# Expert input rows by indirect DMA and transposes instead of gather products, with the gate tiles and the identity moved within SBUF

## The chip, the cores and the metric

The kernel runs on one core of a Trainium2 chip, as one program. The metric is device time in microseconds (us) of one execution, as the median of several runs; lower is better. The core has five engines with a queue each: TensorE (PE, matrix products; its loads of the stationary operand are listed apart as PEld), VectorE (DVE), ScalarE (ACT), GpSimd (POOL) and SyncE (SP, which here only issues DMAs). SBUF is the on-chip memory of 128 partitions; PSUM receives PE's results in banks.

## What is computed

A two-layer trunk on 256 tokens of width 1024 in float32. Layer 0 is a gated spatial mixer followed by a dense SwiGLU. Layer 1 is an attention mixer followed by the part that matters here, a mixture of eight experts where each token goes to two:

```python
def moe_swiglu(x, w_router, w_in, w_out):
    logits = (xt @ w_router)                       # xt: 256 tokens x 1024, RMS-normed
    top_v, top_i = lax.top_k(logits, TOP_K)        # 2 of 8
    top_w = jax.nn.softmax(top_v, axis=-1)
    gates = sum(one_hot(top_i, N_EXPERTS) * top_w) # 256 x 8
    for e in range(N_EXPERTS):
        y = y + gates[:, e:e+1] * swiglu(xt, w_in[e], w_out[e])
```

`w_in[e]` is 1024 x 7168 and `w_out[e]` 3584 x 1024. The eight experts' weights are some 350 of the 459 MB that the program moves.

## The kernel before

**Products in two parts.** All products are made to keep float32 accuracy: each operand is split into a high part (a cast to fp32r) and a low part (the rest), and `mm3` (lines 167 to 171) issues three matmuls, high x weight high (L169), high x weight low (L170), low x weight high (L171). The tokens are the stationary operand (128 x 128), the weights the moving one (128 x 512).

**Weights.** `Stream` fetches weights in units of 128 x 2048 (1 MB) into `w_raw` tiles, issued by SP (L75), up to 9 units ahead in the expert stage. Two halves of each unit are split by ACT (`w_hi`, L91) and DVE (`w_lo`, L100) into a ring of six pairs, from which PE reads. `w_raw` and the other large tiles share one pool of 14 buffers (`big`).

**Experts.** Each expert has a capacity of 128 slots here (a second pass for more than 128 tokens of one expert is behind a branch that is not taken in these runs). `slot` holds the place of each token in each expert. An expert has 14 steps `j`, each over 256 columns of the hidden width: 24 matmuls `mm<-w,xg` (8 chunks of 128 of the input width, three each), SwiGLU on ACT and DVE (`silu` L604, `glu` L605), two transposes of `glu` of the step before (L1177, by the identity tile `ident`), their split into `mgh` on ACT (L1170) and `mgl` on DVE (L1171), and 12 matmuls `acc<-w,mg` into the expert's output. A step reads three units of weights. Program order is written by hand, and every engine works through its queue in that order.

**Input of an expert.** `choose(p)` writes `pick`, the 0/1 matrix (256 tokens x 2 x 128 slots) of a pair of experts, with four DVE instructions (L1128). `gather(p, k)` makes two of the eight chunks of the input of both experts, already transposed: eight matmuls (L1141) with the two parts of the normed tokens (`xnh`, `xnl`) as stationary operand and `pick` moving, 256 columns each, then a cast on ACT (`xgh`, L1144) and a subtraction on DVE (`xgl`, L1145). Four calls make a pair. `slot_info(e)` multiplies `pick` of one expert with `info` (two tiny matmuls, L1150) and so gets each slot's gate, reciprocal norm and token number (`si`, `sg`, L1154 and L1155), and `put` (L1156), a 0/1 matrix of which only the last expert's is read.

**Where these stand.** They go into a list `side`. `pop_side` takes one entry after the 24 `mm` matmuls of a step, one after the first six `acc` matmuls and one after the second six. At step 3 of an odd expert the list gets `choose`, four `gather` and `slot_info` for the next pair, at step 3 of an even expert `slot_info` alone.

**Rows through device memory.** Outputs of experts 0 to 6 are written to a table in device memory (`rows_of`), and four indirect DMAs issued by POOL (`fetch`, L1202) bring each token's two rows back, behind expert 6.

**Before the experts.** `last_out` finishes the attention output, makes the normed tokens `xn` (half 0, then half 1), and calls `parts_of(xn, t)` (lines 966 to 973), which squares `h` on ACT (L316) into a scratch that then receives `xnh`, and makes `xnl`. These tiles are of a pool of four buffers; `xnh` of half 1 takes the buffer that `xn` of half 0 had.

**Addresses.** Nearly all tiles that PE reads start at byte 32 of a 256-byte block of a partition (the large tiles, the weight parts, `gh` and `gl` of the dense layer). `ident`, `mgh` and `mgl` start at byte 160. `phase(nc, pool, size)` allocates padding to set this.

Of the kernel before, what the change touches and what calls it, by code (L numbers as in the profile page):

```python
# [12 lines left out]
F32 = mybir.dt.float32  # L13
F32R = mybir.dt.float32r
# [7 lines left out]
P = 128  # L22
D = 1024
KT = D // P
T = 256
# [97 lines left out]
def phase(nc, pool, size):  # L123


    nc.gpsimd.memset(pool.tile([P, size // 4], F32, name="phase"), 0.0)
# [3 lines left out]
def trunk(ctx: ExitStack, tc: tile.TileContext, a, out):  # L130
# [18 lines left out]
    def aux_bank():  # L149
        return ps_aux.tile([P, 512], F32, name="aux", tag="aux")  # L150
# [4 lines left out]
    def big(dt, name):  # L155
        return bigp.tile([P, BIG], dt, name=name, tag="big")
# [7 lines left out]
    def tok(t):  # L164
        return slice(t * P, (t + 1) * P)
# [83 lines left out]
    units += moe_units(True)  # L249
    ws = Stream(nc, bigp, parts_pool, units, 6)  # L250

    ident = const.tile([P, P], F32, name="ident")
    make_identity(nc, ident)

    wr = const.tile([P, KT * NE], F32, name="wr")
    wr2 = const.tile([P, KT, 2 * NE], F32R, name="wr2")

    def count_up(shape, pattern, base, step, name):
        t = const.tile(shape, F32, name=name)
        nc.gpsimd.iota(t, pattern, base=base, channel_multiplier=step, allow_small_or_imprecise_dtypes=True)  # L260
        return t

    iota_e = count_up([P, NE], [[1, NE]], 0, 0, "iota_e")
    iota_1 = count_up([P, T], [[1, T]], 1, 0, "iota_1")
    number = count_up([P, TT], [[P, TT]], 1, 1, "number")
    strict = const.tile([P, P], BF16, name="strict")
    ones = const.tile([P, P], BF16, name="ones")
    nc.gpsimd.memset(strict, 1.0)
# [37 lines left out]
        for f in todo:  # L306
            f()

    ssh = const.tile([P, TT], F32, name="ssh")
    spare = const.tile([P, 1], F32, name="spare")  # L310
    nc.vector.memset(spare, 0.0)

    def square(t, room=None):
# [647 lines left out]


    xns = {}

    def parts_of(xn, t):

        hi = xnp.tile([P, D], F32R, name="xnh", tag="xn")
        square(t, hi)
        nc.scalar.copy(hi, xn)
        pool, tag = (gains, "gain") if t else (xnp, "xn")  # L970
        lo = pool.tile([P, D], F32R, name="xnl", tag=tag)
        nc.vector.tensor_sub(lo, xn, hi.bitcast(F32))
        xns[t] = hi, lo
# [3 lines left out]
    ws.set_depth(11)  # L977
    pa = ctx.enter_context(tc.tile_pool(name="ma", bufs=1))
    pb = ctx.enter_context(tc.tile_pool(name="mb", bufs=2))
    phase(nc, pa, 64)  # L980
    gate = pa.tile([P, TT, NE], F32, name="gate")
    o1 = pa.tile([P, TT, NE], F32, name="o1m")
    chosen = pa.tile([P, TT, NE], BF16, name="chosen")
# [11 lines left out]
    mostf = pa.tile([P, 1], F32, name="mostf")  # L995
    rm = pa.tile([P, TT], F32, name="rm")
    rms = pa.tile([P, TT, 2], F32R, name="rms")
    s2 = pa.tile([P, TT, 2], F32, name="s2")
    at_row = pa.tile([P, TT, 2], F32, name="at_row")
    fit = pa.tile([P, TT, 2], F32, name="fit")  # L1000
# [1 line left out]
    o1s = pa.tile([P, TT, NE], F32, name="o1s")  # L1002
    place = [pa.tile([P, TT, 2], I32, name=f"place{i}") for i in range(2)]
    nc.gpsimd.memset(nil, 0.0)
    dram = ctx.enter_context(tc.tile_pool(name="dram", bufs=1, space=bass.MemoryType.DRAM))
    nc.gpsimd.memset(info.bitcast(F32), 0.0)


# [105 lines left out]
    def experts(ws, base, before):  # L1114
# [3 lines left out]

        slots = iota_1[:, base : base + P]
        pick, xgs, slot_gate, put, ys, ym, first = {}, {}, {}, {}, {}, {}, {}  # L1120

        def choose(p):

# [6 lines left out]
        def gather(p, k, bank=aux_bank):  # L1130
# [13 lines left out]
            nc.scalar.copy(gh, ps)  # L1144
            nc.vector.tensor_sub(gl, ps, gh.bitcast(F32))  # L1145

        def slot_info(e):
            ps = aux_bank()[:, :6]
            for t in range(TT):
                nc.tensor.matmul(ps, pick[e // 2][:, t, e % 2], info[:, t, e], start=t == 0, stop=t == TT - 1)  # L1150
            si = pb.tile([P, 6], F32, name="si", tag="si")
            slot_gate[e] = pb.tile([P, 2], F32, name="sg", tag="sg")
            put[e] = pb.tile([P, T], F32R, name="put", tag="put")
            nc.vector.tensor_copy(si, ps)  # L1154
            nc.vector.tensor_add(slot_gate[e], si[:, 0:2], si[:, 2:4])  # L1155
            nc.vector.tensor_scalar(put[e], iota_1, si[:, 4:5], None, op0=ALU.is_equal)  # L1156

        def slot_rms():

            ps = aux_bank()[:, :2]  # L1160
            for t in range(TT):
                nc.tensor.matmul(ps, pick[0][:, t, 0], rms[:, t], start=t == 0, stop=t == TT - 1)
            slot_gate[0] = pb.tile([P, 2], F32, name="sg", tag="sg")
            phase(nc, pb, 32)
            nc.vector.tensor_reduce(slot_gate[0][:, 1:2], ps, AX.X, ALU.add)

        def in_parts(pt):
# [115 lines left out]
        for s in range(1 if before else 0, NE * NJ):  # L1283
# [8 lines left out]
                side.append(lambda: slot_info(0))  # L1292
                side.append(lambda: places(0))
            if j == 3 and e < NE - 1:
                if e % 2 == 1:
                    p = e // 2 + 1
                    side.append(lambda p=p: choose(p))
                    side.extend(lambda p=p, k=k: gather(p, k) for k in range(0, KT, 2))
                side.append(lambda e=e: slot_info(e + 1))
            final = s == NE * NJ - 1  # L1300
            for q in range(4):
                w = ws.take(limit=4 if final else N_PARTS)
                for k2 in range(2):
                    k = 2 * q + k2
                    x = tuple(g[:, k, cs] for g in xgs[e // 2])
                    mm3(ps, x, cols(w, k2 * 512, (k2 + 1) * 512), k == 0, k == KT - 1)
                if q == 0 and s == 2 and before:
                    gT0 = first_rows()
                if q == 1 and prev is not None:
                    gT = transposed_m(prev[3])  # L1310
                if q == 3:
                    pop_side()
# [85 lines left out]
```

## Time and profile before

| | us |
|---|---|
| median of 3 runs (1568.2 to 1569.3) | 1568.31 |
| profiled execution, its own time | 1570.13 |
| span of its records | 1567.8 |
| PE busy | 1547.5 |
| DVE busy | 1271.3 |
| ACT busy | 1058.1 |

The profiled execution took 1.8 us more than the median, and 2.3 us of it lie outside its span. The expert stage runs from about 586 us to the end, and PE's granted clock is 1.00 of full speed in it. In the rows, the start of an instruction is in us from the span's start; a matmul's recorded duration includes its way through the array, so that successive matmuls overlap. The distance from one start to the next is what a matmul costs PE.

### The profile page before, as it was taken

How to read it: one execution, taken by the hardware profiler on the slowest of the kernel's cores; microseconds unless marked ns; L12 is line 12 of the kernel's file. 1: busy time of each engine (PE TensorE's matmuls, PEld its weight loads, DVE VectorE, ACT ScalarE, POOL GpSimd, SP SyncE). 2: the span in 40 equal slices, each digit the busy share in tenths (PEclk: the TensorE clock that was granted, in tenths of full speed). 3: DMA queues.
4: the chain of work that ended last, by engine and by line, in shares of the span. 5: the costliest groups of instructions: out<-in, count | busy, mean ns of one | idle time of the engine just before them, and what ended most of it. 6: DMA issues, size and time to landing. Idle time of an engine off the chain costs nothing.

```text
span 1567.8 us, 20336 instructions
## 1 busy us (share of the span) xinstructions
PE 1547.5 (99%) x7389; PEld 1288.3 (82%) x7389; DVE 1271.3 (81%) x1636; ACT 1058.1 (67%) x1403; POOL 48.4 (3%) x76
## 2 busy tenths in 40 slices
PE   9999999999999999999999999999999999999997
PEld 8999988888889777888888888888888888888875
DVE  6576666555786679999999999999999998998996
ACT  6555544444556657777777777777778777777774
POOL 1000000000100520000000000000000000000100
PEclk9999999999999999999999999999999999999999
DMA  9465648552333558998999998999998999999980
GB/s 379 138 208 194 237 174 339 184 188 81 126 148 135 189 215 319 377 365 316 352 371 367 419 385 315 342 367 361 420 385 314 349 374 383 372 412 338 396 355 29
DMA packets 70172, 459.30 MB, mean 293 GB/s; under 512 B 8032, under 2 KB 10096, under 8 KB 19376
## 3 DMA queue, kind: packets, MB, share of 16 engines
q1 hardware_dynamic: 67104, 451.97, 75.5%
q10 hardware_dynamic: 2160, 3.68, 0.6%
q0 software_dynamic: 800, 2.28, 0.5%
q8 instruction: 60, 0.98, 0.3%
q14 instruction: 48, 0.39, 0.1%
HBM read 453.17 MB, written 4.72 MB: 292 GB/s over the span
## 4 chain that ended last, share of the span: by engine, by line
PE 60%; DVE 2%; issue 1%; ACT 1%; DVEq 0%; ACTq 0%
PE mm L169 13%; PE mm L171 13%; PE mm L170 12%; PE acc L169 7%; PE acc L171 7%; PE acc L170 6%; PE aux L1177 2%; DVE w_lo L100 1%; PE aux L1141 1%; ACT w_hi L91 0%; PE acc L1141 0%; DVE h L1210 0%; DVE h L1217 0%; DVE mgl L1171 0%; DVE pick L1128 0%
## 5 line engine op out<-in xcount | busy, mean ns | idle before, releaser
L100 DVE TENSOR_TENSOR w_lo<-w_raw,w_hi 128x1024 fp32r<-128x1024 f32 (+1 forms) x858 | 993.4, 1202 | 163.9 <-ACT w_hi L91 152.2
L91 ACT CAST w_hi<-w_raw 128x1024 fp32r<-128x1024 f32 (+1 forms) x866 | 848.4, 1033 | 102.6 <-PE acc L171 61.6
L169 PE MATMUL mm<-w_hi,xgh 128*128 128x512 f32 x880 | 356.3, 405 | 0.0
L171 PE MATMUL mm<-w_hi,xgl 128*128 128x512 f32 x880 | 346.1, 393 | 0.0
L170 PE MATMUL mm<-w_lo,xgh 128*128 128x512 f32 x880 | 342.5, 389 | 0.0
L171 PEld LDWEIGHTS mm<-w_hi,xgl 128*128 128x128 f32 x880 | 165.1, 188 | 38.8
L170 PEld LDWEIGHTS mm<-w_lo,xgh 128*128 128x128 f32 x880 | 165.8, 188 | 32.9
L169 PEld LDWEIGHTS mm<-w_hi,xgh 128*128 128x128 f32 x880 | 165.2, 188 | 31.0
L169 PE MATMUL acc<-w_hi,mgh 128*128 128x512 f32 x448 | 177.8, 397 | 0.5 <-ACT mgh L1170 0.5
L171 PE MATMUL acc<-w_hi,mgl 128*128 128x512 f32 x448 | 176.8, 395 | 1.4 <-DVE mgl L1171 1.4
L170 PE MATMUL acc<-w_lo,mgh 128*128 128x512 f32 x448 | 177.1, 395 | 0.0
L1170 ACT CAST mgh<-aux 128x256 fp32r<-128x256 f32 x112 | 41.7, 373 | 153.5 <-PE aux L1177 153.5
L171 PEld LDWEIGHTS acc<-w_hi,mgl 128*128 128x128 f32 x448 | 84.5, 189 | 22.3 <-DVE mgl L1171 2.3
L170 PEld LDWEIGHTS acc<-w_lo,mgh 128*128 128x128 f32 x448 | 84.6, 189 | 19.1 <-DVE w_lo L100 0.3
L169 PEld LDWEIGHTS acc<-w_hi,mgh 128*128 128x128 f32 x448 | 84.2, 188 | 19.3 <-ACT mgh L1170 0.7
L604 ACT ACTIVATE silu<-mm,sg 128x256 f32<-128x256 f32 x110 | 52.1, 474 | 53.7 <-PE mm L171 48.8
L169 PE MATMUL mm<-w_hi,xfh 128*128 128x512 f32 x160 | 63.3, 396 | 0.0
L171 PE MATMUL mm<-w_hi,xfl 128*128 128x512 f32 x160 | 62.4, 390 | 0.0
L170 PE MATMUL mm<-w_lo,xfh 128*128 128x512 f32 x160 | 62.3, 390 | 0.0
L170 PE MATMUL mm<-w_lo,xah 128*128 128x384 f32 x176 | 59.1, 336 | 0.4 <-DVE w_lo L100 0.4
L169 PE MATMUL mm<-w_hi,xah 128*128 128x384 f32 x176 | 59.4, 337 | 0.1
L171 PE MATMUL mm<-w_hi,xal 128*128 128x384 f32 x176 | 59.0, 335 | 0.1
(367 smaller groups left out, 1846.1 us busy)
## 6 DMA issues: line engine op xcount, KB each, us to landing
w_raw<-in_m_in SPq DMA_DIRECT2D x224, 1024.0 KB, 6.8
w_raw<-in_m_out SPq DMA_DIRECT2D x111, 1024.0 KB, 7.1
w_raw<-in_a_in SPq DMA_DIRECT2D x31, 768.0 KB, 9.4
w_raw<-in_f_in SPq DMA_DIRECT2D x22, 1024.0 KB, 5.8
w_raw<-in_f_out SPq DMA_DIRECT2D x11, 1024.0 KB, 5.0
w_raw<-in_a_out SPq DMA_DIRECT2D x8, 1024.0 KB, 6.4
w_raw<-in_kv_in SPq DMA_DIRECT2D x8, 1024.0 KB, 4.7
w_raw<-in_a_out SPq DMA_DIRECT2D x8, 512.0 KB, 4.6
```

Source lines behind the costliest of these rows:

```text
L91: self.nc.scalar.copy(hi[:, :n], src)
L100: (low or self.low).tensor_sub(lo[:, :n], src, hi[:, :n].bitcast(F32))
L169: nc.tensor.matmul(o, x[0], w[0], start=start, stop=False)
L170: nc.tensor.matmul(o, x[0], w[1], start=False, stop=False)
L171: nc.tensor.matmul(o, x[1], w[0], start=False, stop=stop)
L604: nc.scalar.activation(s, ps[:, 0:256], AF.Silu, scale=r)
L1141: nc.tensor.matmul(ps[:, k2], lhs, rhs[t], start=i == 0, stop=i == 3)
L1170: nc.scalar.copy(gh, pt)
L1177: nc.tensor.transpose(pt[:, k], g[:, k * P : (k + 1) * P], ident)
```

## The change

Experts 0 and 1 keep the gather products. For experts 2 to 7:

- `parts_of` also writes each half of the normed tokens `xn` to a table `x_rows` in device memory, with one plain DMA of 512 KB issued by POOL. The buffer of `xn` of half 0 is next written by the square of half 1 on ACT, which therefore waits for that DMA.
- `choose_one(e)` writes `pick` for one expert (two DVE instructions); `slot_info(e)` also makes `token`, the slots' token numbers as integers, and `put` is made for the last expert alone.
- `fetch_x(e)` reads the 128 rows of 4 KB with an indirect DMA issued by POOL, into a `big` tile `xrow`.
- `turn_x(e, b)`, twice, transposes four 128 x 128 blocks each with PE, casts them on ACT and subtracts on DVE. `xe` (both parts, one `big` tile) takes the place of `xg`.
- At step 3 of every expert but 0 and 7 the list gets `choose_one`, `slot_info`, `fetch_x`, four empty entries and two `turn_x`.

Of the addresses: `iota_e`, `number`, `ssh` and `spare` are allocated ahead of `ident`, and a padding is halved and another dropped. By the built program's allocation `ident` moves from byte 160 to byte 32 of 256, and `mgh` and `mgl`, in all steps of all experts, too.

```diff
+    iota_e = const.tile([P, NE], F32, name="iota_e")
+    number = const.tile([P, TT], F32, name="number")
+    ssh = const.tile([P, TT], F32, name="ssh")
+    spare = const.tile([P, 1], F32, name="spare")
     ident = const.tile([P, P], F32, name="ident")
...
+    x_rows = dram.tile([T, D], F32, name="x_rows")
     def parts_of(xn, t):
+        nc.gpsimd.dma_start(x_rows[tok(t), :], xn)
         hi = xnp.tile([P, D], F32R, name="xnh", tag="xn")
...
-    phase(nc, pa, 64)
+    phase(nc, pa, 32)
...
+        def choose_one(e):
+            pick[e // 2] = pb.tile([P, TT, 2, P], F32R, name="pick", tag="pick", bufs=1)
+            for t in range(TT):
+                nc.vector.tensor_scalar(
+                    pick[e // 2][:, t, e % 2], slots, slot[:, t, e : e + 1], None, op0=ALU.is_equal
+                )
+        def fetch_x(e):
+            xr_[e] = big(F32, "xrow")
+            nc.gpsimd.indirect_dma_start(
+                out=xr_[e][:, :D],
+                out_offset=None,
+                in_=x_rows[:, :],
+                in_offset=bass.IndirectOffsetOnAxis(ap=token[e], axis=0),
+            )
+        def turn_x(e, b):
+            if b == 0:
+                x2 = big(F32R, "xe")[:, :UNIT].rearrange("p (i k n) -> p i k n", i=2, k=KT)
+                xes[e] = x2[:, 0], x2[:, 1]
+            pt = aux_bank().rearrange("p (k n) -> p k n", k=4)
+            for k in range(4):
+                nc.tensor.transpose(pt[:, k], xr_[e][:, (4 * b + k) * P : (4 * b + k + 1) * P], ident)
+            gh, gl = (g[:, 4 * b : 4 * b + 4] for g in xes[e])
+            nc.scalar.copy(gh, pt)
+            nc.vector.tensor_sub(gl, pt, gh.bitcast(F32))
         def slot_info(e):
...
-            put[e] = pb.tile([P, T], F32R, name="put", tag="put")
             nc.vector.tensor_copy(si, ps)
             nc.vector.tensor_add(slot_gate[e], si[:, 0:2], si[:, 2:4])
-            nc.vector.tensor_scalar(put[e], iota_1, si[:, 4:5], None, op0=ALU.is_equal)
+            if e >= 2:
+                token[e] = pb.tile([P, 1], I32, name="token", tag="token")
+                nc.vector.tensor_scalar(token[e], si[:, 4:5], -1.0, 0.0, ALU.add, ALU.max)
+            if e == LAST:
+                put[e] = pb.tile([P, T], F32R, name="put", tag="put")
+                nc.vector.tensor_scalar(put[e], iota_1, si[:, 4:5], None, op0=ALU.is_equal)
...
-            slot_gate[0] = pb.tile([P, 2], F32, name="sg", tag="sg")
-            phase(nc, pb, 32)
+            slot_gate[0] = r0
...
             if j == 3 and e < NE - 1:
-                if e % 2 == 1:
-                    p = e // 2 + 1
-                    side.append(lambda p=p: choose(p))
-                    side.extend(lambda p=p, k=k: gather(p, k) for k in range(0, KT, 2))
-                side.append(lambda e=e: slot_info(e + 1))
+                if e > 0:
+                    side.append(lambda f=e + 1: choose_one(f))
+                side.append(lambda f=e + 1: slot_info(f))
+                if e > 0:
+                    side.append(lambda f=e + 1: fetch_x(f))
+                    side.extend([lambda: None] * 4)
+                    side.extend(lambda f=e + 1, b=b: turn_x(f, b) for b in range(2))
...
-                    x = tuple(g[:, k, cs] for g in xgs[e // 2])
+                    x = tuple(g[:, k] for g in xes[e]) if e > 1 else tuple(g[:, k, cs] for g in xgs[0])
```

On PE, at step 3 of expert 1, the order before has the first gather of the next pair between the two sixes of `acc` matmuls (the piece ends behind the first four of its eight matmuls):

```order
L171 MATMUL acc_6506<-w_hi_6747,mgl_6773 128x512
L1141 MATMUL aux_6819<-pick_6798,xnh_5161 128x256
L1141 MATMUL aux_6819<-pick_6798,xnl_5164 128x256
L1141 MATMUL aux_6819<-pick_6798,xnh_5258 128x256
L1141 MATMUL aux_6819<-pick_6798,xnl_5261 128x256
```

Three more such pieces follow at the next places. In the order of the changed kernel the same place holds the two matmuls of `slot_info` (its line is now 1183):

```order
L171 MATMUL acc_6503<-w_hi_6744,mgl_6770 128x512
L1183 MATMUL aux_6812<-info_5198,pick_6795 128x6 x2
L169 MATMUL acc_6502<-w_hi_6754,mgh_6769 128x512
L170 MATMUL acc_6502<-w_lo_6755,mgh_6769 128x512
L171 MATMUL acc_6502<-w_hi_6754,mgl_6770 128x512
```

and on PE two steps later, at step 5 of the same expert, stand the eight transposes of the fetched rows, in two runs of four:

```order
L171 MATMUL acc_6503<-w_hi_6914,mgl_6940 128x512
L1175 MATMUL aux_6980<-ident_117,xrow_6833 128x128 x4
L169 MATMUL acc_6502<-w_hi_6924,mgh_6939 128x512
L170 MATMUL acc_6502<-w_lo_6925,mgh_6939 128x512
L171 MATMUL acc_6502<-w_hi_6924,mgl_6940 128x512
L169 MATMUL acc_6503<-w_hi_6924,mgh_6939 128x512
L170 MATMUL acc_6503<-w_lo_6925,mgh_6939 128x512
L171 MATMUL acc_6503<-w_hi_6924,mgl_6940 128x512
L1175 MATMUL aux_6999<-ident_117,xrow_6833 128x128 x4
```

So 32 matmuls of 256 columns per pair of experts left PE's queue and 8 transposes per expert came in. On DVE, before, at the same step 3 of expert 1, `pick` has four instructions and the first two evacuations of the gather follow:

```order
L100 TENSOR_TENSOR w_lo<-w_raw,w_hi 128x1024 x2
L1128 TENSOR_SCALAR pick<-iota_122,slot 128x128 x4
L605 SCALAR_TENSOR_TENSOR glu<-mm,sg,silu 128x256
L100 TENSOR_TENSOR w_lo<-w_raw,w_hi 128x1024
L1145 TENSOR_TENSOR xgl<-aux,xgh 128x512
```

In the changed kernel DVE has there two instructions for `pick`, and behind `glu` and one `w_lo` the three that end in `token`, for which POOL's fetch waits:

```order
L100 TENSOR_TENSOR w_lo<-w_raw,w_hi 128x1024 x2
L1154 TENSOR_SCALAR pick<-iota_124,slot 128x128 x2
L604 SCALAR_TENSOR_TENSOR glu<-mm,sg,silu 128x256
L100 TENSOR_TENSOR w_lo<-w_raw,w_hi 128x1024
L1186 COPY si<-aux 128x6
L1187 TENSOR_TENSOR sg<-si 128x2
L1190 TENSOR_SCALAR token<-si 128x1
L100 TENSOR_TENSOR w_lo<-w_raw,w_hi 128x1024 x3
```

So what follows `pick` on DVE no longer waits for a gather, and `token` comes one `w_lo` later.

## Rows read from the trace of the kernel before

**Rows 1.** Page, part 1: busy us (share of the span) and instructions by engine.

```profile
PE 1547.5 (99%) x7389; PEld 1288.3 (82%) x7389; DVE 1271.3 (81%) x1636; ACT 1058.1 (67%) x1403; POOL 48.4 (3%) x76
```

**Rows 2.** Waits of PE, the longest: us in total, times, longest us.

```profile
PE mm L882 <- DVE work L877: 3.2, 3, 1.4
```

**Rows 3.** Windows cut at a step's first matmul: length, busy by engine, clock, DMA.

```profile
725.77:755.85 30.08, 29.95 (x150) 24.83 (x148) 27.70 (x37) 21.82 (x29) 0.00 (x0) 1.00 0.91 349
755.85:841.21 85.36, 85.36 (x382) 69.40 (x380) 77.71 (x81) 65.25 (x81) 0.00 (x0) 1.00 0.99 378
849.76:867.04 17.28, 17.28 (x80) 14.11 (x79) 16.29 (x21) 13.05 (x17) 0.00 (x0) 1.00 1.00 414
```

**Rows 4.** Timeline of PE at the first gather of a pair: start, duration.

```profile
732.66 0.40 PE L171 MATMUL acc<-w_hi,mgl 128*128 128x512 f32 x1
733.20 0.36 PE L1141 MATMUL aux<-pick,xnh 128*128 128x256 f32 x1
...
734.32 0.39 PE L169 MATMUL acc<-w_hi,mgh 128*128 128x512 f32 x1
```

**Rows 5.** Timeline of DVE at the same place and at the following slot_info.

```profile
732.57 0.87 DVE L1128 TENSOR_SCALAR pick<-iota,slot 128x128 fp32r<-128x128 f32 x4
...
733.75 1.22 DVE L100 TENSOR_TENSOR w_lo<-w_raw,w_hi 128x1024 fp32r<-128x1024 f32 x1
...
748.61 0.16 DVE L1154 COPY si<-aux 128x6 f32<-128x6 f32 x1
```

**Rows 6.** Timeline of PE: four transposes of xn between matmuls.

```profile
567.71 0.39 PE L171 MATMUL mm<-w_hi,xrl 128*128 128x512 f32 x1
567.94 0.60 PE L334 MATMUL aux<-ident,xn 128*128 128x128 f32 x4
568.29 0.48 PE L169 MATMUL mm<-w_hi,xrh 128*128 128x512 f32 x1
568.61 0.40 PE L170 MATMUL mm<-w_lo,xrh 128*128 128x512 f32 x1
```

**Rows 7.** Lines, the transposes of glu: count, busy us, mean ns of one.

```profile
L1177 PE MATMUL aux<-ident,glu 128*128 128x128 f32 x222 | 42.2, 271 | 1.4 <-DVE glu L605 1.4
```

**Rows 8.** Timeline of PE, a step of expert 2 without side work.

```profile
755.85 0.40 PE L169 MATMUL mm<-w_hi,xgh 128*128 128x512 f32 x1
...
756.54 0.40 PE L169 MATMUL mm<-w_hi,xgh 128*128 128x512 f32 x1
756.78 0.39 PE L170 MATMUL mm<-w_lo,xgh 128*128 128x512 f32 x1
...
758.37 0.39 PE L171 MATMUL mm<-w_hi,xgl 128*128 128x512 f32 x1
...
761.58 0.40 PE L169 MATMUL acc<-w_hi,mgh 128*128 128x512 f32 x1
...
764.38 0.40 PE L169 MATMUL mm<-w_hi,xgh 128*128 128x512 f32 x1
```

**Rows 9.** Timeline of PE in the dense layer: first of 18 acc matmuls, and what follows them.

```profile
299.76 0.39 PE L169 MATMUL acc<-w_hi,gh 128*128 128x512 f32 x1
...
303.84 0.39 PE L169 MATMUL mm<-w_hi,xfh 128*128 128x512 f32 x1
```

**Rows 10.** Source line 1202, the four indirect DMAs: ns min/median/max, and landing.

```profile
L1202 POOL DMA_INDIRECT got<-rows_of,place x4: 937/948/1662, 1451.5 to 1455.9; - x4
...
DMA to landing us min/median/max: 8.6/11.3/15.2
```

**Rows 11.** Window over these four DMAs, columns as in rows 3.

```profile
1451.00:1459.00 8.00, 8.00 (x37) 6.54 (x36) 8.00 (x10) 7.15 (x9) 4.49 (x4) 1.00 0.94 345
```

**Rows 12.** Timeline of DVE at parts_of: half 0 of xn is done.

```profile
561.15 0.69 DVE L321 TENSOR_TENSOR xn<-h,gain 128x512 f32<-128x512 f32 x1
```

**Rows 13.** Timeline of ACT at parts_of: the square of half 1.

```profile
571.10 1.06 ACT L316 ACTIVATE xnh<-h 128x1024 fp32r<-128x1024 f32 x1
```

**Rows 14.** DMA issues: KB each, median us to landing.

```profile
gain<-in_f_g SPq DMA_DIRECT2D x1, 512.0 KB, 6.9
```

More of the change, by code (lines that the diff above doesn't have):

```diff
@@ L256, in trunk @@
     wr2 = const.tile([P, KT, 2 * NE], F32R, name="wr2")
-    def count_up(shape, pattern, base, step, name):
-        t = const.tile(shape, F32, name=name)
+    iota_1 = const.tile([P, T], F32, name="iota_1")
+    for t, pattern, base, step in (
+        (iota_e, [[1, NE]], 0, 0), (iota_1, [[1, T]], 1, 0), (number, [[P, TT]], 1, 1)
+    ):
         nc.gpsimd.iota(t, pattern, base=base, channel_multiplier=step, allow_small_or_imprecise_dtypes=True)
[L261 to L265, printed above, removed]
     strict = const.tile([P, P], BF16, name="strict")
@@ L307, in rsqrt @@
             f()
-    ssh = const.tile([P, TT], F32, name="ssh")
-    spare = const.tile([P, 1], F32, name="spare")
     nc.vector.memset(spare, 0.0)
@@ L963, in trunk @@
     xns = {}
+    dram = ctx.enter_context(tc.tile_pool(name="dram", bufs=1, space=bass.MemoryType.DRAM))
+    x_rows = dram.tile([T, D], F32, name="x_rows")
     def parts_of(xn, t):
+        nc.gpsimd.dma_start(x_rows[tok(t), :], xn)
         hi = xnp.tile([P, D], F32R, name="xnh", tag="xn")
@@ L997, in trunk @@
     rms = pa.tile([P, TT, 2], F32R, name="rms")
+    r0 = pa.tile([P, 2], F32, name="r0")
     s2 = pa.tile([P, TT, 2], F32, name="s2")
@@ L1004, in trunk @@
     nc.gpsimd.memset(nil, 0.0)
-    dram = ctx.enter_context(tc.tile_pool(name="dram", bufs=1, space=bass.MemoryType.DRAM))
     nc.gpsimd.memset(info.bitcast(F32), 0.0)
@@ L1120, in experts @@
         pick, xgs, slot_gate, put, ys, ym, first = {}, {}, {}, {}, {}, {}, {}
+        token, xr_, xes = {}, {}, {}
         def choose(p):
```

## The prediction

> **What bounds the kernel now.** I read the page's busy times first: PE is busy for 1547.5 of 1567.8 us [rows 1], with DVE next at 1271.3. Then PE's waits: the longest sum is 3.2 us, in the attention stage, and nothing in the expert stage comes near [rows 2]. Then the steps of the experts, in windows cut at the first matmul of a step: ten steps without side work take 85.36 us with PE busy for all of it [rows 3], so 8.536 us a step. DVE is busy for 77.7 of these 85.4 us and ACT for 65.3, so both have room, but DVE has little (0.77 us a step). The weights keep up: they arrive at 378 GB/s in these steps, and at 414 GB/s in another stretch [rows 3], so that DMA has some 10% left where it is asked. So what PE no longer does in the expert stage comes off the end, as long as DVE, ACT and the fetches keep up, and each matmul's spacing counts, over 1344 `acc` and some 2650 `mm` matmuls.
>
> **The gather products that go.** The three steps that hold one pair's gather and the `slot_info` behind it take 30.08 us [rows 3]; three plain steps take 3 x 8.536 = 25.61, so these cost 4.47. The two steps around a lone `slot_info` take 17.28, which is 0.21 above two plain ones [rows 3]. The gather of a pair, with PE's wait for `pick` in it, is then 4.26 us, and three pairs are **-12.8 us**. That stands to the matmuls themselves: eight take 733.20 to 734.32 [rows 4], 1.12 us with the first two held a little by `pick`, and four times that is 4.5.
>
> **The transposes that come.** Four transposes between two matmuls move the start of the next but one from 567.71 to 568.61, 0.90 us, where two plain spacings take about 0.46 [rows 6, 8]: 0.44 us for four, 0.11 each. Six experts with two runs of four: 12 x 0.44 = **+5.3 us**. Their casts and subtractions are as many and as large as those of the gathers (two of 128 x 512 an expert, where a pair had four), so ACT and DVE do the same work, spread over six places instead of three; `put` goes for six and `token`, a tiny one, comes for six. I cost these at nothing: DVE's 0.77 us a step and the six parts ahead of PE hide them, as they hid the gathers'.
>
> **The wait for `pick`.** Before, the first gather came 0.54 us after the matmul ahead of it [rows 4], 0.31 above the usual 0.23, because DVE began `pick` only at 732.57 [rows 5]. Three such waits are inside the 12.8. Now two of the four DVE instructions are needed, but the waiting matmuls load `pick` as stationary operand, and this comes at six experts instead of three. DVE writes two in about 0.48 us (four take 0.87 [rows 5]), to 733.05; the first gather started 0.15 to 0.2 us after its part was done, and a load takes about 0.2, which puts the second small matmul at 733.4 instead of 733.0. That is 0.4 us for six: **+2.4 us**, between nothing and 2.7. Queued behind it on PE are the second six `acc` matmuls of that step; no one else waits for it.
>
> **The fetch.** No trace shows this one, only its like: POOL needs 0.95 to 1.7 us to issue, and the rows land 8.6 to 15.2 us after the issue began, for four in a row beside the weights [rows 10]. A single one should be like the first, 8.6. The time it has: counted from the start of step 3, `pick` is at 6.8, the `w_lo` behind it ends at 9.2 [rows 5], `si`, `sg` and `token` take 0.16 each [rows 5], so POOL starts at about 9.9; the first transpose stands two places past two more step starts, at 2 x 8.5 + 7.2 = 24.3. So 14.4 us are there and 8.6 are needed: nothing is added. Past 14.4 each further us costs 6. POOL has nothing else queued behind the fetches until those of the output rows, and its engine time is otherwise 48 us [rows 1].
>
> **Writing the rows.** The write of half 0 is issued when DVE ends `xn` at 561.84 [rows 12]; 512 KB landed in 6.9 us elsewhere [rows 14], so about 570 with POOL's issue. ACT's square of half 1, which waits for it, began at 571.10 [rows 13]. About 1 us to spare; were it 2 us late, the two units of parts that are ahead of PE there would carry most of it. Nothing to 2 us; I take nothing.
>
> **The addresses.** In one plain step the 12 `acc` matmuls, with `mgh` and `mgl` at byte 160, take 761.58 to 764.38: 0.2333 us each. Eleven `mm` matmuls of the same step, with the tokens at byte 32, take 755.85 to 758.37: 0.2291 [rows 8]. In the dense layer 18 `acc` matmuls, with `gh` and `gl` at byte 32, take 299.76 to 303.84: 0.2267 [rows 9]. If the byte is the reason, 1344 `acc` matmuls gain 0.0042 each, **-5.6 us**, by the nearest row (same step, same load of ACT and DVE); -8.9 by the dense layer's. If it is not, 0. Below nothing: single spacings at byte 32 in that step reach 0.24 (756.54 to 756.78 [rows 8]); were all `acc` at 0.236, it would be +3.6. I take -5.6. For `ident` I take nothing, as transposes are few.
>
> **The sum.** -12.8 + 5.3 + 2.4 - 5.6 = -10.7. The profiled execution took 1570.1, so 1559.4 there; it was 1.8 above the median, so **1557.6 us** as a median.
>
> **Rivals.**
> *The byte does nothing.* The spacings differ by something else (which engine reads or writes beside them). Then -5.1: 1563.2. For it: single spacings at byte 32 vary as much as the difference. Against it: three rows agree in order.
> *Byte 32 is worse*, because the gates then start where the weight parts start: -5.1 + 3.6 = -1.5, 1566.8, no change that can be measured. Against it: the dense layer's row.
> *A transpose costs its recorded time.* The row gives a mean of 271 ns [rows 7]; 48 of them are 13.0 in place of 5.3, and the sum -3.0: 1565.3. Against it: four start to start within 0.44 [rows 6], and these are the same 128 x 128 of float32. The Trainium skill (TensorE: Matmul & The Clock Gate, Part 4: PE-mode transpose) gives about 275 ns for one in a kernel, and by that price the exchange would bring nothing; this trace agrees with 275 as the length of one, not as what one costs in a run.
> *The fetch lands late.* At the first `turn_x` PE waits, with all of the expert's matmuls behind it. It makes the kernel slower by over 0.2% (3.1 us) from (10.7 + 3.1) / 6 = 2.3 us of lateness, so from a landing at 16.7 us. At twice the first fetch's 8.6, 17.2, it is 6 x 2.8 = +16.8, and 1574.4. For it: the fourth of the four took 15.2 [rows 10]. Against it: that one stood behind three others. POOL's part can be held up as well: these four were issued in 0.95 us each, the first in 1.7, while DVE was busy for all of the 8 us around them [rows 11]. The Trainium skill (SBUF — State Buffer, Who interferes with whom) says that POOL cannot write descriptors while DVE runs an instruction in a two-port mode; by that a fetch would wait for the end of such an instruction, and the trace shows no more than the 0.7 us of the first.
>
> **How the numbers follow.** The likeliest (exchange as summed, byte as in rows 8) has 0.57; the byte nothing 0.25; byte worse 0.05; transposes at their length 0.05; late fetch 0.06; something better, as the dense layer's spacing, 0.02. About 0.2% is what a measurement of this kernel can tell from no change, so faster means below 1565.2. Faster 0.57 + 0.25 + 0.02 and a little of the transposes: 0.85; same 0.09; slower 0.06. The range reaches from the likeliest with the dense layer's spacing and no wait for `pick` (-12.8 + 5.3 - 8.9 = -16.4, 1552) to the case where the byte does nothing, with a wait of 2.7 and 1.5 for the write of the rows (-3.3): 1565.0.
>
> **What would show it.** Right: PE still shows no wait at the transposes; the three steps 3 to 5 of an expert at about 27.0 (25.6 + 0.4 + 0.2 + 0.9, less 0.15 of spacing); `acc` spacing at 0.229; the fetch landing within 14 us of its issue. Wrong: a wait of PE for `xrow`, or `acc` spacing at 0.233 as before, or a plain step longer than 8.54 because DVE no longer keeps up with PE.

## The result, and the profile after

The changed kernel takes **1550.76 us** (median of 4 runs, 1550.03 to 1551.14), beside 1568.52 before on the same chip: a ratio of 0.9885, 95% interval 0.9868 to 0.9903. That is 17.8 us less, where 10.7 were forecast; it lies 1.2 us under the range. Its profiled execution took 1551.14 us, with a span of 1549.4.

The page's busy times, PE again in front of the others, answer to [rows 1]:

```profile
PE 1529.7 (99%) x7341; PEld 1280.4 (83%) x7341; DVE 1267.7 (82%) x1635; ACT 1058.7 (68%) x1403; POOL 57.6 (4%) x83
```

PE has 48 matmuls fewer and is busy 17.8 us less, so the whole gain is time that PE no longer spends on matmuls. Its waits, the three longest (us in total, times, longest), answer to [rows 2]; none is for `xrow`:

```profile
PE mm L881 <- DVE work L876: 3.2, 3, 1.4
PE aux L1213 <- DVE glu L604: 1.4, 1, 1.4
PE acc L171 <- DVE mgl L1207: 1.4, 2, 1.0
```

Windows cut as in [rows 3]: the ten plain steps between the exchange for expert 2 and that for expert 3, the ten that follow the latter, and the four steps with the exchange for expert 3.

```profile
758.44:842.77 84.33, 84.33 (x381) 69.29 (x380) 77.34 (x81) 66.44 (x83) 0.00 (x0) 1.00 0.97 378
877.92:962.06 84.14, 84.14 (x382) 69.32 (x380) 77.35 (x81) 66.49 (x83) 0.00 (x0) 1.00 0.94 366
842.77:877.92 35.15, 35.15 (x163) 28.68 (x162) 33.54 (x40) 27.29 (x35) 1.21 (x1) 1.00 1.00 406
```

A plain step is 8.433 or 8.414 us, 8.424 on average, against 8.536: over 112 steps 12.5 us. The exchange of an expert costs 35.15 - 4 x 8.433 = 1.42 us; six are 8.5, where the three pairs with their lone `slot_info` cost 3 x (4.47 + 0.21) = 14.0 before: 5.5 us less. The two make up the 17.8 within 0.2. So the exchange gave what was forecast for it (5.1), and the steps gave twice as much.

A plain step of expert 2 on PE's timeline (start, duration), beside [rows 8], whose step is by its place step 6 of expert 1 and not one of expert 2: the first and the twelfth `mm`, the first `acc`, and the next step's first `mm`.

```profile
877.92 0.39 PE L169 MATMUL mm<-w_hi,xe 128*128 128x512 f32 x1
...
880.42 0.39 PE L171 MATMUL mm<-w_hi,xe 128*128 128x512 f32 x1
...
883.62 0.39 PE L169 MATMUL acc<-w_hi,mgh 128*128 128x512 f32 x1
...
886.34 0.39 PE L169 MATMUL mm<-w_hi,xe 128*128 128x512 f32 x1
```

The twelve `acc` take 2.72 us, 0.2267 each (0.2333 before), and the eleven spacings of `mm` 2.50, 0.2273 each (0.2291 before). Both are faster, though the bytes of the tokens are the same as before.

The exchange itself. PE and then DVE at the first `slot_info` with its `pick`, beside [rows 4, 5]:

```profile
730.16 0.39 PE L171 MATMUL acc<-w_hi,mgl 128*128 128x512 f32 x1
730.53 0.38 PE L1183 MATMUL aux<-info,pick 128*128 128x6 f32 x2
730.77 0.48 PE L169 MATMUL acc<-w_hi,mgh 128*128 128x512 f32 x1
```

```profile
730.11 0.48 DVE L1154 TENSOR_SCALAR pick<-iota,slot 128x128 fp32r<-128x128 f32 x2
```

PE's four transposes of `xrow`, beside [rows 6]:

```profile
747.50 0.39 PE L171 MATMUL acc<-w_hi,mgl 128*128 128x512 f32 x1
747.73 0.60 PE L1175 MATMUL aux<-ident,xrow 128*128 128x128 f32 x4
748.09 0.48 PE L169 MATMUL acc<-w_hi,mgh 128*128 128x512 f32 x1
748.40 0.40 PE L170 MATMUL acc<-w_lo,mgh 128*128 128x512 f32 x1
```

The first fetch on POOL's timeline, and the source line of all six (ns min/median/max, and landing), beside [rows 10]:

```profile
733.29 1.24 POOL L1161 DMA_INDIRECT xrow<-x_rows,token  x1 [142.26 <-DMA w_raw<-in_m_in]
```

```profile
L1161 POOL DMA_INDIRECT xrow<-x_rows,token x6: 1117/1206/1383, 733.3 to 1330.1; - x6
...
DMA to landing us min/median/max: 9.3/9.6/10.7
```

The first fetch is issued at 733.29 and used at 747.73: 14.4 us of room, as worked out beforehand, for a landing of 9.3 to 10.7.

### The profile page after: what moved, and what is told of

Read it like the earlier page. It is cut to its first block, busy times and chain, and to the rows that moved or that the text cites. A ratio compares the mean times of both kernels' runs of the same rounds, so it can differ in the third digit from the quotient of the medians.

```text
span 1549.4 us, 20282 instructions
## 1 busy us (share of the span) xinstructions
PE 1529.7 (99%) x7341; PEld 1280.4 (83%) x7341; DVE 1267.7 (82%) x1635; ACT 1058.7 (68%) x1403; POOL 57.6 (4%) x83
## 4 chain that ended last, share of the span: by engine, by line
PE 59%; DVE 2%; issue 1%; ACT 0%; DVEq 0%; ACTq 0%
PE mm L171 13%; PE mm L169 13%; PE mm L170 13%; PE acc L169 6%; PE acc L171 6%; PE acc L170 6%; PE aux L1213 2%; DVE w_lo L100 1%; PE aux L1175 0%; DVE h L1246 0%; PE acc L1144 0%; ACT w_hi L91 0%; PE aux L1183 0%; DVE glu L604 0%; DVE h L1253 0%
## 5 line engine op out<-in xcount | busy, mean ns | idle before, releaser
L169 PE MATMUL mm<-w_hi,xe 128*128 128x512 f32 x672 | 269.9, 402 | 0.0
L171 PE MATMUL mm<-w_hi,xe 128*128 128x512 f32 x672 | 263.0, 391 | 0.0
L170 PE MATMUL mm<-w_lo,xe 128*128 128x512 f32 x672 | 262.1, 390 | 0.0
L171 PEld LDWEIGHTS mm<-w_hi,xe 128*128 128x128 f32 x672 | 126.1, 188 | 27.3
L170 PEld LDWEIGHTS mm<-w_lo,xe 128*128 128x128 f32 x672 | 126.6, 188 | 24.0
L169 PEld LDWEIGHTS mm<-w_hi,xe 128*128 128x128 f32 x672 | 126.2, 188 | 23.5
L169 PE MATMUL mm<-w_hi,xgh 128*128 128x512 f32 x208 | 83.7, 402 | 0.0
L171 PE MATMUL mm<-w_hi,xgl 128*128 128x512 f32 x208 | 81.4, 391 | 0.0
L170 PE MATMUL mm<-w_lo,xgh 128*128 128x512 f32 x208 | 81.2, 390 | 0.0
```

What stands on the lines that cost most here:

```text
L169: nc.tensor.matmul(o, x[0], w[0], start=start, stop=False)
L170: nc.tensor.matmul(o, x[0], w[1], start=False, stop=False)
L171: nc.tensor.matmul(o, x[1], w[0], start=False, stop=stop)
```

## The experiments

Four theories stand at the start. G: the start byte of the gates `mgh` and `mgl` sets the spacing of the `acc` that load them, and of the `mm` behind these. I: it is the byte of `ident`. S: steps are shorter because the gathers are gone. And the forecast's own term, `acc` alone from 0.2333 to 0.2291.

**e1_gates160: the gates back at byte 160.** A small weight tile moves out of the constants to make room, and 128 bytes are put ahead of the gates.

```diff
-    wr = const.tile([P, KT * NE], F32, name="wr")
+    def router_weights(pool):
+        wr = pool.tile([P, KT * NE], F32, name="wr")
...
         def first_rows():
+            phase(nc, pb, 64)
```

> The kernel after, with the tiles mgh and mgl alone back at byte 160 of 256 (ident stays at 32). In the traces a plain step is 8.424 us after and 8.536 before, an acc matmul 0.227 and 0.233. Theory G, the start byte of mgh and mgl sets the spacing of the acc matmuls that load them, and of the first mm matmuls behind them: acc 0.233, plain step 8.536, 112 steps x 0.112 = +12.5 us, 1563.3. Theory I, it is the byte of ident (two transposes in every step): as after, 1550.8, acc 0.227. Theory S, the steps are shorter because the gathers are gone, not by a byte: 1550.8 too.

**e2_ident160: `ident` back at byte 160.**

```diff
+    ident = const.tile([P, P], F32, name="ident")
+    make_identity(nc, ident)
     iota_e = const.tile([P, NE], F32, name="iota_e")
     number = const.tile([P, TT], F32, name="number")
     ssh = const.tile([P, TT], F32, name="ssh")
     spare = const.tile([P, 1], F32, name="spare")
-    ident = const.tile([P, P], F32, name="ident")
-    make_identity(nc, ident)
```

> The kernel after, with ident (and the router's weights and four small tiles around it) alone back at byte 160; mgh and mgl stay at 32. Theory G: as after, 1550.8, acc 0.227, plain step 8.42. Theory I: acc 0.233, plain step 8.536, 1563.3. Theory S: 1550.8.

**e3_bytes: the bytes alone, on the kernel before** (the small tiles around `ident` move with it).

```diff
+    iota_e = const.tile([P, NE], F32, name="iota_e")
...
     ident = const.tile([P, P], F32, name="ident")
...
-    phase(nc, pa, 64)
+    phase(nc, pa, 32)
...
+    r0 = pa.tile([P, 2], F32, name="r0")
...
-            slot_gate[0] = pb.tile([P, 2], F32, name="sg", tag="sg")
-            phase(nc, pb, 32)
+            slot_gate[0] = r0
```

> The kernel before with the bytes alone changed: ident, mgh and mgl at byte 32, the gather products kept. Theories G and I: plain step 8.42, 1568.5 - 12.5 = 1556.0. By the prediction's own term for the addresses (acc 0.229): 1562.9. Theory S: 1568.5, acc 0.233.

**e4_both160: the exchange alone**, the edits of e1_gates160 and e2_ident160 together.

> The exchange alone: the rows fetched and transposed as in the kernel after, ident, mgh and mgl at byte 160 as before. Theories G and I: plain step 8.536, and the exchange as the two traces show it (per expert 1.43 us after, 4.47 for a pair and 0.21 for each lone slot_info before: 8.6 against 14.0), 1568.5 - 5.4 = 1563.1. Theory S: 1550.8.

Measured, beside 1569.22 for the kernel before; the step is the mean of the ten plain steps whose window stands below the table:

| kernel | gates, `ident` | us (runs) | ratio to before | plain step |
|---|---|---|---|---|
| e1_gates160 | 160, 32 | 1560.46 (1560.19 to 1561.49) | 0.9944 [0.9928, 0.9961] | 8.526 |
| e2_ident160 | 32, 160 | 1550.94 (1550.79 to 1552.36) | 0.9885 [0.9869, 0.9902] | 8.427 |
| e3_bytes | 32, 32, gathers kept | 1556.24 (1555.48 to 1557.39) | 0.9916 [0.9899, 0.9932] | 8.413 |
| e4_both160 | 160, 160 | 1563.11 (1562.09 to 1564.68) | 0.9959 [0.9945, 0.9973] | 8.538 |

The windows of ten plain steps, one fence a kernel, in that order:

```profile
880.72:965.98 85.26, 85.26 (x381) 69.40 (x380) 77.56 (x81) 66.44 (x83) 0.00 (x0) 1.00 0.95 360
```

```profile
878.35:962.62 84.27, 84.27 (x381) 69.36 (x380) 77.40 (x81) 66.46 (x83) 0.00 (x0) 1.00 0.96 367
```

```profile
871.77:955.90 84.13, 84.13 (x382) 69.30 (x380) 77.62 (x81) 65.41 (x81) 0.00 (x0) 1.00 0.98 389
```

```profile
882.92:968.30 85.38, 85.38 (x381) 69.48 (x380) 77.58 (x81) 66.45 (x83) 0.00 (x0) 1.00 0.94 359
```

Theory G holds and S falls: the bytes alone give 13.0 us, the exchange alone 6.1, and the two add up to the result within 1.3 us. Putting the gates back costs 9.7 us of the gain (1560.46 against 1550.76), where 12.5 had been expected of it. `ident` does nothing by itself (0.2), so theory I falls too, but it costs 2.65 us on top of the gates (1563.11 against 1560.46), which no theory had foretold; the plain steps hold about half of that (8.538 against 8.526, 1.3 us over 112). DVE is busy for 77.4 to 77.6 us in all these windows and ACT for 65.4 to 66.5, the least of it in a fast one (e3_bytes) and the same in e1_gates160 and e2_ident160, so it is not their load.

**e5_xe_scan: is it any loaded tile?** The tokens of six experts at six bytes. (This run and the next five, to e8_room, were executed once each; the conclusions rest on spacings and waits of their traces, which come again from step to step.)

```diff
+XE_BYTE = {e: (b - 32) % 256 // 4 for e, b in {2: 160, 3: 0, 4: 64, 5: 96, 6: 128, 7: 224}.items()}
...
-                x2 = big(F32R, "xe")[:, :UNIT].rearrange("p (i k n) -> p i k n", i=2, k=KT)
+                o = XE_BYTE[e]
+                x2 = big(F32R, "xe")[:, o : o + UNIT].rearrange("p (i k n) -> p i k n", i=2, k=KT)
```

> The kernel after, with the tokens xe of experts 2 to 7 starting at bytes 160, 0, 64, 96, 128 and 224 of 256, one byte an expert (0 and 1 keep byte 32). In the kernel after the mm matmuls that load them at byte 32 take 0.2267 each where nothing disturbs them. Theory G widened, any tile that a matmul loads counts by its byte: expert 2's mm go to about 0.233, its plain step from 8.43 to about 8.43 + 24 x 0.009 = 8.65, by the gates' 0.11 for 12. Rival, it is the place of the gates next to the small tiles and not a byte: all experts at 8.41 to 8.43. What the other bytes give is not known; a rule 'only the byte of the weight parts, 32, is fast' would slow all six.

Windows of two plain steps each: an expert at byte 32 first (gathered, as before), then bytes 160, 0, 64, 96, 128 and 224.

```profile
665.26:682.08 16.82, 16.82 (x77) 13.87 (x76) 15.60 (x17) 13.06 (x17) 0.00 (x0) 1.00 0.98 373
887.84:904.87 17.03, 17.03 (x78) 13.90 (x76) 15.62 (x17) 13.04 (x17) 0.00 (x0) 1.00 0.99 382
1017.12:1034.20 17.08, 17.08 (x77) 13.85 (x76) 15.62 (x17) 13.05 (x17) 0.00 (x0) 1.00 1.00 377
1138.08:1155.16 17.08, 17.08 (x78) 13.87 (x76) 15.63 (x17) 13.07 (x17) 0.00 (x0) 1.00 0.97 361
1259.17:1276.32 17.15, 17.15 (x77) 13.88 (x76) 15.63 (x17) 13.04 (x17) 0.00 (x0) 1.00 0.98 375
1380.64:1397.83 17.19, 17.19 (x77) 13.88 (x76) 15.63 (x17) 13.06 (x17) 0.00 (x0) 1.00 1.00 378
...
1457.41:1474.32 16.91, 16.91 (x77) 13.87 (x76) 15.63 (x17) 13.07 (x17) 0.00 (x0) 1.00 1.01 415
```

A step is 8.52 to 8.60 us at five of the bytes and 8.45 at 224 (1560.58 us in all). So the tokens count as the gates do. At byte 160 the cost was about half of the 0.22 that was expected: 24 `mm` a step share some 0.1 us. The first eleven start 233 ns apart, as the `acc` did with gates at 160; those behind the two transposes start late at byte 32 too (see below), and lose less.

**e6_gate_scan: fourteen bytes for the gates** (the weights get one large buffer less).

```diff
+G_BYTE = 0, 16, 32, 48, 64, 80, 96, 112, 128, 144, 160, 176, 192, 224
...
+                if j == 0:
+                    rooms[e] = big(F32R, "mg")
+                o = (G_BYTE[2 * e - 2 + j // 7] - 32) % 256 // 4 + j % 2 * 4 * P
```

> The kernel after, with the gates of experts 1 to 7 in a large tile, at fourteen start bytes, one for seven steps each: 0, 16, 32, 48, ... 192 and 224 of 256. Theory 'upper half': plain steps of 8.41 to 8.43 at 0 to 112, of 8.53 at 128 to 224. Theory 'same byte as the weight parts': 8.41 to 8.43 at byte 32 alone, 8.53 at all others. Rival, it is the place and not the byte: all fourteen alike.

**e7_parts160: the streamed weight parts at byte 160**, everything else at 32 as in the kernel after.

```diff
+    pad2 = ctx.enter_context(tc.tile_pool(name="pad2", bufs=1))
+    phase(nc, pad2, 128)
     parts_pool = ctx.enter_context(tc.tile_pool(name="parts", bufs=N_PARTS))
...
-    phase(nc, pads, 64)
+    phase(nc, pads, 192)
```

> The kernel after, with the weight parts w_hi and w_lo, which the matmuls stream, at byte 160 instead of 32; gates, tokens and ident stay at 32. If the byte of the loaded tile alone counts: as after, 1550.8, acc 0.227. If the distance between the loaded tile and the parts counts: acc and mm both at about 0.233 from the first product with parts on, some 6500 x 0.006 = +39 us.

**e9_scan_parts160: both at once**, the fourteen bytes of e6_gate_scan with the parts of e7_parts160.

> The gates at the same fourteen bytes as in the run e6_gate_scan, but the weight parts at byte 160 instead of 32. There, with the parts at 32, acc was 0.2267 at bytes 16, 32, 48 and 176, 0.229 at 224 and 0.232 to 0.234 at the nine others. Theory D, the distance from the parts' byte to the loaded tile's counts (fast at -16, 0, +16 and +144): fast now at 144, 160, 176 and 48, slow at 16 and 32; 0.229 at 96. Theory A, the loaded tile's own byte counts, and the parts' byte by itself too: 16, 32, 48 and 176 are still the faster ones, and 144 and 160 the slower. The mm are slow under both, as in e7_parts160 (0.232), so the time itself tells nothing: about 1575 to 1580.

e7_parts160 took 1575.5 us, 24.7 more than the kernel after; its ten plain steps:

```profile
768.93:854.80 85.87, 85.87 (x382) 69.56 (x380) 77.66 (x81) 66.44 (x83) 0.00 (x0) 1.00 0.95 370
```

That is 8.587 a step, 0.163 more: the streamed tile's byte counts as well, so the loaded tile's own byte can't be the whole rule. (39 us had been expected of a rule by distance; the steps carry 18 of the 24.7, and the trace of the kernel after has some 5500 matmuls of this shape where 6500 were assumed.) e6_gate_scan took 1557.0, e9_scan_parts160 1575.26. Spacing of the `acc` in ns, the mean of twelve, median of the undisturbed plain steps at that byte (4 to 7 of them):

| byte of the gates | 0 | 16 | 32 | 48 | 64 | 80 | 96 | 112 | 128 | 144 | 160 | 176 | 192 | 224 |
|---|---|---|---|---|---|---|---|---|---|---|---|---|---|---|
| parts at 32 | 232.7 | 226.7 | 226.7 | 226.7 | 232.9 | 232.8 | 233.2 | 231.7 | 234.0 | 233.0 | 233.0 | 226.7 | 233.2 | 229.0 |
| parts at 160 | 234.0 | 232.6 | 232.5 | 227.2 | 233.5 | 230.4 | 229.8 | 233.3 | 233.1 | 228.4 | 227.3 | 227.2 | 232.7 | 233.1 |

In e6_gate_scan 16, 32, 48 and 176 are fast, so both rules on record for it fall, the one by halves and the one by byte 32 alone, and so does their rival, that all bytes are alike.

The crossing in rows of PE: the first `acc` of a step and the `mm` that follows the twelfth. Parts at 32, gates at 32 and then at 160:

```profile
832.54 0.39 PE L172 MATMUL acc<-w_hi,mg 128*128 128x512 f32 x1
...
835.26 0.39 PE L172 MATMUL mm<-w_hi,xe 128*128 128x512 f32 x1
...
1313.46 0.40 PE L172 MATMUL acc<-w_hi,mg 128*128 128x512 f32 x1
...
1316.26 0.40 PE L172 MATMUL mm<-w_hi,xe 128*128 128x512 f32 x1
```

Parts at 160, gates at 32 and then at 160:

```profile
853.03 0.40 PE L174 MATMUL acc<-w_hi,mg 128*128 128x512 f32 x1
...
855.83 0.39 PE L174 MATMUL mm<-w_hi,xe 128*128 128x512 f32 x1
...
1338.37 0.39 PE L174 MATMUL acc<-w_hi,mg 128*128 128x512 f32 x1
...
1341.09 0.40 PE L174 MATMUL mm<-w_hi,xe 128*128 128x512 f32 x1
```

2.72 and 2.80, then 2.80 and 2.72: the same two bytes change places when the parts move by 128. That is theory D, the distance between the loaded and the streamed tile; theory A falls. The other columns go with it (16 and 144 change places, 96 and 224 too, and 80 and 112 with the parts at 160, 230.4 and 233.3, stand beside 229.9 and 231.5 at 208 and 240 in e10_fine_scan below), with a rest: with the parts at 160 the steps at bytes 48 and 176 were partly 227 and partly 233. There the `mm` ahead of the `acc` are slow too, which may carry over.

**e10_fine_scan: finer steps, and the period.** As e6_gate_scan, with other bytes.

```diff
-G_BYTE = 0, 16, 32, 48, 64, 80, 96, 112, 128, 144, 160, 176, 192, 224
+G_BYTE = 4, 8, 12, 24, 40, 56, 60, 168, 184, 208, 240, 288, 304, 416
```

> As e6_gate_scan (parts at 32), with the gates at bytes 4, 8, 12, 24, 40, 56, 60, 168, 184, 208, 240, 288, 304 and 416. If the pattern repeats every 256 bytes, 288 and 304 are as fast as 32 and 48 (0.2267) and 416 as slow as 160 (0.2323). If the fast bytes are a window about the parts' byte, 24 and 40 are fast, 4 to 12 and 56 to 60 show its edges, and 168 and 184 those of the second one at 176.

It took 1558.9 us. `acc` spacing: 226.7 at bytes 4, 60, 288 and 304; 231.3, 231.5, 233.2, 231.0, 231.0 at 8, 12, 24, 40, 56; 232.6, 230.8, 229.9, 231.5 at 168, 184, 208, 240; 233.0 at 416. So the pattern repeats after 256 bytes (288 and 304 are as 32 and 48, 416 as 160). But the fast bytes are no window: 24 and 40, eight bytes from the parts' 32, are slow, while 4 and 60 are fast. Why just these is open. What holds in every run is that the same byte for both is fast (226.7 ns at 32, 227 to 228 at 160).

**e8_room: is the fetch hidden by its room alone?** Three of the four empty places go.

```diff
-                    side.extend([lambda: None] * 4)
+                    side.append(lambda: None)
```

> The kernel after, with three of the four empty places between a row fetch and its transposes taken out, so that the transposes stand one step (8.4 us) earlier. In the trace of after the first fetch is issued 14.4 us ahead of its first transpose and lands 9.3 us from its issue. If the fetch is hidden by that room alone, PE now waits 9.3 - 6.0 = 3.3 us and up to 4.7 at the later ones, for six experts: +20 to +28 us, 1571 to 1579. If the rows land earlier than the record of the transfer says, or PE makes it up: under +10.

1571.99 us, 21.2 more than after, though the rows land a little sooner here (7.9 to 9.6 us). PE's longest wait, the stretches around two of the six transposes and two short windows in the second (columns as in [rows 3]; the last but two is the granted clock), and PE's timeline in the second:

```profile
PE aux L1175 <- DMA xrow<-x_rows,token: 14.9, 6, 3.4
```

```profile
854.76:874.39 19.63, 17.97 (x86) 14.56 (x84) 16.99 (x20) 13.75 (x19) 1.21 (x1) 1.00 1.00 396
975.85:998.81 22.96, 19.60 (x86) 15.77 (x84) 17.09 (x20) 13.73 (x19) 1.20 (x1) 0.93 0.86 332
988.00:990.00 2.00, 2.00 (x6) 1.41 (x6) 1.59 (x2) 1.07 (x2) 0.00 (x0) 0.52 0.17 70
990.00:992.00 2.00, 2.00 (x13) 1.69 (x12) 1.02 (x2) 1.46 (x3) 0.00 (x0) 1.00 0.46 66
```

```profile
986.44 1.07 PE L1175 MATMUL aux<-ident,xrow 128*128 128x128 f32 x4 [3.36 <-DMA xrow<-x_rows,token]
987.16 0.77 PE L169 MATMUL acc<-w_hi,mgh 128*128 128x512 f32 x1
987.73 0.63 PE L170 MATMUL acc<-w_lo,mgh 128*128 128x512 f32 x1
988.16 0.63 PE L171 MATMUL acc<-w_hi,mgl 128*128 128x512 f32 x1
```

With 14.4 - 8.4 = 6.0 us of room and a landing of 8.6 (median), PE waits 2.5 us on average: the fetch is hidden by its room and by nothing else. The six stretches are together 20.8 us longer than the 17.77 of the kernel after, but only 14.9 of that is waiting. Most of the rest is the clock: behind three of the six waits (3.36, 2.66 and 2.33 us) the matmuls start 0.43 apart for some 3 us, at a granted clock of about 0.5, which is the level of 1.2 GHz, and PE is busy for 19.4 to 19.6 us instead of 17.97, together 4.7 us more. Behind the other three (2.47, 2.42 and 1.66) it was not, so the length of the wait alone does not decide. The last 1.2 us are 0.2 in each of the six, where PE is busy for 17.97 instead of 17.77 without a lower clock.

**e11_small: the two waits of the side work that are left.** `choose_one` one place earlier, and `add_got` in halves with an empty place behind each.

```diff
                     side.append(lambda f=e + 1: choose_one(f))
+                    side.append(lambda: None)
...
-                    side.extend([lambda: None] * 4)
+                    side.extend([lambda: None] * 3)
...
-                    r += [lambda t=t, i=i: add_got(t, i) for t, i in ti]
+                    r += [f for t, i in ti for b in range(2) for f in (lambda t=t, i=i, b=b: add_got(t, i, b), lambda: None)]
```

> The kernel after with the two waits of the side work that its trace still shows taken away: the two instructions that write pick one place earlier (slot_info stands 0.37 us behind its neighbour after, 0.23 would be no wait: 6 x 0.14), and add_got in halves with an empty place behind each (the one step with it takes 10.05 us after, a plain one 8.41). If both go: 1550.8 - 0.84 - 1.64 = 1548.3. If the additions only move their wait to other steps: 1549.9.

**1547.69 us** (1546.98 to 1549.21), a ratio to before of 0.9862, interval 0.9846 to 0.9878: ahead of both kernels, by 3.1 us of the kernel after, with no overlap of the runs (3.5 if each is taken from the kernel before beside it). `slot_info` now starts a usual spacing behind its neighbour, and the matmul behind its two follows 0.14 us later (0.24 in the kernel after):

```profile
732.26 0.39 PE L171 MATMUL acc<-w_hi,mgl 128*128 128x512 f32 x1
732.49 0.28 PE L1183 MATMUL aux<-info,pick 128*128 128x6 f32 x2
732.63 0.48 PE L169 MATMUL mm<-w_hi,xgh 128*128 128x512 f32 x1
```

The four steps with the exchange for expert 3, in the kernel after 35.15 us, and the step with the additions, first in the kernel after:

```profile
843.25:878.14 34.89, 34.89 (x164) 28.73 (x162) 33.47 (x40) 27.31 (x35) 1.13 (x1) 1.00 1.00 407
```

```profile
1473.11:1483.16 10.05, 9.02 (x39) 6.85 (x38) 10.05 (x12) 7.43 (x9) 0.00 (x0) 1.00 1.01 417
```

```profile
1472.31:1480.72 8.41, 8.41 (x39) 6.93 (x38) 8.40 (x11) 6.53 (x9) 0.00 (x0) 1.00 1.01 418
```

The wait for `pick` was worth 0.26 us an expert and not the 0.14 that was expected, so 1.6 us for six beside the 1.64 of the additions; that is why the time came out 0.6 under the expected 1548.3.

## Why the prediction was wrong

**What bounds the kernel: right.** PE was busy throughout and nothing else became late; the whole gain is on PE.

**The exchange: right, 5.5 us by the trace for 5.1.** By runs it is 6.1 with the old bytes (e4_both160) and 5.5 with the new ones (e3_bytes to the kernel after). The transposes cost 747.50 to 748.40, 0.90 us with two plain spacings of 0.227 in it, so 0.45 for four, as forecast; the rival that prices one at its recorded 271 ns [rows 7] is out. The wait for `pick` came out smaller, 0.24 us an expert where 0.4 was put. The first small matmul needs one of DVE's instructions and started 0.42 us after DVE began (the first gather, which needs two, 0.63 [rows 4, 5]): 0.37 - 0.23 = 0.14. The second waited too: the next `acc` follows 0.24 behind the first, where the two without a wait take 0.14 (e11_small), so 0.10 more. That is 6 x 0.16 = 1.0 us of the forecast's error. The other way goes what the forecast left out: of the 1.42 us an expert, 0.90 are the transposes, 0.24 the wait and 0.21 `slot_info`, and 0.07 is left, 0.4 us for six. The trace shows most of it: behind each four transposes the five matmuls that follow the first one start 224 to 236 ns apart, 0.03 us late in all, before the spacing is 226.7 again.

**The fetch and the writing of the rows: right.** The room was 14.4 us to the tenth; the landing 9.3 to 10.7 instead of 8.6. POOL took 1.12 to 1.38 us to issue with DVE busy around it, so no fetch was held up for longer than in [rows 10]. e8_room shows what stood behind the rival of the late fetch, and that its price was too low: it counted each us of lateness as one, and the steps grew by 20.8 for 14.9 of waiting, 4.7 of it by the clock. The two writes landed 2.9 and 6.9 us after their issue, the first of them issued at 561.47, and ACT's square of half 1, which waits for it, began at its usual place (0.67 us sooner than before, as all of this stage):

```profile
570.43 1.06 ACT L315 ACTIVATE xnh<-h 128x1024 fp32r<-128x1024 f32 x1
```

**The addresses: this step failed.** It took -5.6 "by the nearest row (same step, same load of ACT and DVE)", from `acc` at 0.2333 against `mm` at 0.2291. Measured: 13.0 us by e3_bytes, 12.4 by e4_both160 to the kernel after. Three things were wrong with it.

First, the nearest row was not undisturbed. Of the 0.112 us that a step gains from the gates' byte alone (8.526 to 8.414), 0.076 lies in the twelve `acc` (233.0 to 226.7 ns) and most of the rest in the `mm` right behind them. These load tokens at byte 32 in both kernels, and start 236, 224, 231, 236, 228, 232 and 231 ns apart behind gates at 160 (means over the plain steps of e1_gates160), then 226.7. So the 0.2291 of the eleven `mm` [rows 8] was itself an effect of what it was compared with. The dense layer's row [rows 9], 0.2267, was the right one: no slow matmul is ahead of it. The forecast named it, as the end of the range, with a chance of 0.02 and for the `acc` alone.

Second, only the `acc` were counted. With all of a step's matmuls the dense layer's row gives 12 x (0.2333 - 0.2267) + 11 x (0.2291 - 0.2267) = 0.106 us a step, and 11.8 us over 112 steps. The sum would have been -16.9, against the measured -17.8.

Third, `ident` was put at nothing, "as transposes are few". It is nothing with the gates at 32, but 2.65 us with the gates at 160.

**The rivals.** "The byte does nothing" fell with e3_bytes. "Byte 32 is worse, because the gates then start where the weight parts start" had cause and sign exactly the wrong way round: e7_parts160 and e9_scan_parts160 show that starting where the parts start is one of the fast distances.

**What stays open.** The rows show that PE's spacing depends on the distance; they don't show how. The recorded weight loads are no help. The likely place is that the load of one matmul runs beside the streaming of the one before, and that the two reads meet; this is argued only. Plain steps after the change are 8.414 us between one exchange and the next and 8.433 between that one and the one after it, by the late matmuls behind the two transposes of `glu` (five in the one case, nine in the other); why they alternate is open too (some 1 us in all).

## What to carry to other kernels

Before a spacing is taken as the undisturbed one, look at what runs ahead of it: take the row from a stretch in which the suspected cause is absent altogether, and not from its neighbour, and then count every instruction whose spacing differs from that row. Where PE is the bound, start the tiles that its matmuls load at the same byte modulo 256 as the tiles that they stream; here this was measured for 512-column products of float32 parts, and for no other. And a transfer that is hidden by room alone costs its lateness, and perhaps the clock on top, as soon as the room is gone.

## What the runs showed of the hardware

- The distance between the start bytes of the loaded and the streamed tile, modulo 256, changes the spacing of 512-column matmuls: 226.7 ns at the same byte, 229 to 234 at most others, with a pattern that is no window (0, 16, 28 and 144 bytes apart are fast, 8, 20, 24 and 32 slow). The Trainium skill (TensorE: Matmul & The Clock Gate, Step-by-step: what each phase is for) says that loading the next tile's weights takes no SBUF read bandwidth from the running matmul. At the fast distances the rows agree; at the others a matmul starts 2 to 7 ns later, and if that is the load, which no run shows, the sentence does not hold there. The Trainium skill (SBUF — State Buffer, Who interferes with whom) also says that PE never waits on anyone; these runs moved only what PE itself reads and do not test that.
- A delay of the `acc` is not over with them: behind gates at 160 the next seven `mm` still start late, by 4 ns on average (e1_gates160). Transposes leave the same kind of tail, also with everything at byte 32: behind the first matmul that follows them, five to nine spacings of 224 to 236 ns (the kernel after).
- Behind a wait of 2.3 to 3.4 us the granted clock can fall to its lower level for some 3 us; of six waits of 1.7 to 3.4 us in e8_room three did it (2.33, 2.66 and 3.36), and 2.42 and 2.47 did not.
